# One pipe for both halves of a differential attention, and its rope and transposes allowed to start earlier

## The chip, the cores and the metric

The kernel runs on one core of one Trainium2 chip. The metric is device time in microseconds (us) of that core for one launch: the median of the runs shown. In the profile PE is TensorE (PEld its weight loads), DVE VectorE, ACT ScalarE, POOL GpSimd, and SP the engine that issues most of the DMAs.

## The reference, cut to what matters

The program computes two transformer blocks for 256 tokens of width 2048, all in fp32. What the change touches lies in the first block:

```python
h = rms_norm(x, g) * (1 + scale_a) + shift_a          # modulation from w_ada
proj = h @ w_in                                       # d_q d_k d_v | s_q s_k s_v | i_q i_k i_w
# differential attention: 8 heads, two 64-wide q/k per head, v 128 wide, causal, rope on q and k
p1 = softmax(mask(q1 @ k1.T) / 8);  p2 = softmax(mask(q2 @ k2.T) / 8)
diff_out = rms_norm((p1 - lam * p2) @ v, g_sub) * 0.2
# selected-key attention: 8 heads of 128 share one k and v; an index score picks 64 keys per query
dsa_out = softmax(where(selected, s_q @ s_k.T, -inf) / sqrt(128)) @ s_v
x = x + gate_a * rms_norm(concat(diff_out, dsa_out) @ w_o)
# then the gated feed-forward of this block, and the second block
```

## The kernel before, in words

**Weights.** Every projection streams its fp32 weights from HBM in pieces of up to 1 MB. A piece is loaded by SP into a buffer of a ring (`pump_dma`, L242 to L268); then, in units of two 128-row chunks, ACT copies it to a rounded part `wh` (L286) and DVE computes the rest `wl` (L287), and PE multiplies `hi*wh + hi*wl + lo*wh` (L327 to L329). A split is written at most `LOOK = 3` units ahead of the unit that PE works on (L273). The modulation needs `w_ada`, whose pieces PE reads as loaded (`ada`, L650); the planner deals them between the projections (`merge`, L349).

**The ring.** It has four fixed buffers (`raw0` to `raw3`) and up to `lent["max"]` more (tile name `rawb`), lent from the 14 big tiles (`slots`). A buffer comes back when its last unit is split, or when PE has read a modulation piece (`release`, L216). When a big tile is asked for and none is free, a lent one is reclaimed (L79).

**The order of the work.** Nothing is scheduled at run time: the Python program writes every engine's instructions in their final order, driven by a model clock that PE instructions advance (L64, L69). Side work (attention, evictions, norms) is written as generators that `yield` a model time until their next piece. `pipe` (L366) lays items through stages: item i reaches stage j at model time i*every + offs[j].

**The attentions.** `dsa_gen` (L897) sends 8 items (2 query tiles, 4 head pairs) through stages sA to sE; PE scores and adds the mask, DVE and ACT make the softmax, PE transposes `p` and multiplies with v. `diff_gen` (L961) waits for all of `dsa`, then, for each half q (4 heads), allocates and clears `kTz` (POOL memset, L1047), ropes `accA` on DVE (L1052), transposes k and q on PE (L1055, L1059) and evicts them to `kTz` and `dqT`, and sends 8 items through its seven stages: sA scores (`sc<-kTz,dqT`), sB softmax, sC the combination of p1 and p2 on DVE (L989, L990), sD transposes of `p`, sE the product with v (`tp<-accV,pt`), sF the norm, sG transposes of `osb`. The second half begins with nothing until the first pipe has drained and freed `kTz0`. Meanwhile PE works through the rest of `w_in` (tiles `h1h`, `h1l`), then `w_o`, first the selected-key rows (`mh`, `ml`), then the differential rows, which need `diff` (L1205).

Of the kernel before, what the change touches and what calls it, by code (L numbers as in the profile page):

```python
# [10 lines left out]
R32 = mybir.dt.float32r  # L11
BF = mybir.dt.bfloat16
I32 = mybir.dt.int32
AF = mybir.ActivationFunctionType
# [3 lines left out]
P = 128  # L18
# [21 lines left out]
def kernel(ctx: ExitStack, tc: tile.TileContext, a, freq, out):  # L40
# [30 lines left out]

    T = PE

    # ------------------------------------------------------------------ storage
    slots = deque(range(14))
    slot_of = {}

    def big(name, shape=(P, 8, 256), dt=F32):
        if not slots:  # L79
            reclaim()  # L80
        i = slots.popleft()
        t = bigp.tile(list(shape), dt, name=name, tag=f"b{i}")
        slot_of[name] = i
        return t

    def free(*names):
        for n in names:
            slots.append(slot_of.pop(n))
# [30 lines left out]
    def sc_bank():  # L119
        return psx.tile([P, 512], F32, name="sc", tag="sc", bufs=2)  # L120

    # ------------------------------------------------------------------ driver
    bg = []
    H = {}

# [9 lines left out]
    def spawn(gen, name=None):  # L135
        h = Handle()
        if name is not None:
            H[name] = h
        e = [gen, clock["t"], h]
        if step_gen(e):  # L140
            bg.append(e)
        return h
# [10 lines left out]
    def mark(name):  # L153
        H[name] = Handle()
        H[name].done = True
# [10 lines left out]
    def done(*names):  # L166
        return all(x in H and H[x].done for x in names)
# [29 lines left out]
                     "fin": u["last"] == i} for i, (u, ts) in enumerate(seq)]  # L197

    ring = deque(("raw", i) for i in range(N_RAW))
    lent = {"now": 0, "max": 0}  # L200

    def reclaim():
        for r in ring:
# [7 lines left out]
    def lend(n):  # L211
        lent["max"] = n
        while lent["now"] > n and reclaim():
            pass

    def release(it):  # L216
        ring.append(it["res"])
        lend(lent["max"])

    def run(steps):  # L220
# [21 lines left out]
        def pump_dma():  # L242
            while pos["dma"] < len(items):
                i = pos["dma"]
                it = items[i]
                if lent["now"] < lent["max"] and len(slots) > 0:
                    ring.append(("big", slots.popleft()))
                    lent["now"] += 1
                if not ring:
                    return  # L250
                it["res"] = ring.popleft()
                if it["res"][0] == "raw":
                    it["tile"] = rawp.tile([P, 2048], F32, name="raw", tag=f"raw{it['res'][1]}")
                else:
                    it["tile"] = bigp.tile([P, 2048], F32, name="rawb", tag=f"b{it['res'][1]}")
                if it["kind"] == "w":
                    g = it["grp"]
                    kcs = it["kcs"]
                    r0 = kcs[0] * P
                    src = g.w[r0:r0 + len(kcs) * P, g.c0:g.c0 + g.n].rearrange("(c p) n -> p c n", p=P)  # L260
                    it["view"] = it["tile"][:, :len(kcs) * g.n].rearrange("p (c n) -> p c n", n=g.n)
                    nc.sync.dma_start(it["view"], src)
                else:
                    it["load"](it["tile"])
                nb = 2048 if it["kind"] == "ada" else len(it["kcs"]) * it["grp"].n
                pos["t"] = max(pos["t"], clock["t"]) + nb * 512 / 361e3
                it["due"] = pos["t"] + DLAT
                pos["dma"] += 1  # L268
# [94 lines left out]
    def call(fn):  # L363
        return {"kind": "call", "fn": fn}

    def pipe(items, stages, offs, every):  # L366
        ev = sorted((i * every + offs[j], -j, i) for i in range(len(items)) for j in range(len(stages)))
        t = 0.0
        for tt, j, i in ev:
            if tt > t:  # L370
                yield tt - t
                t = tt
            stages[-j](items[i])

    # ------------------------------------------------------------------ constants
    v1 = wtile(tag="P", bufs=4, name="v1")
    v1 = v1[:, :P]
    rows = lambda v, n: v.rearrange("o (r c) -> (o r) c", c=P)[:n]
# [125 lines left out]
        V.tensor_scalar(nlam, nlam, 0.2, None, op0=OP.subtract)  # L504


    # ------------------------------------------------------------------ helpers
    def rstd_of(ssq, n, width, name="rstd"):
        k = ssq.shape[1]
        v = small(k, name + "v")  # L510
# [10 lines left out]
    def quad_transpose(src, pb=None):  # L521
        pb = pb if pb is not None else tp_bank()
        n = src.shape[1] // P
        for j in range(n):
            T.transpose(pb[:, j * P:(j + 1) * P], src[:, j * P:(j + 1) * P], ident)
        return pb[:, :n * P].rearrange("p (c q) -> p c q", q=P)
# [25 lines left out]
            A.activation(h, src, AF.Copy, scale=scale)  # L552
            V.scalar_tensor_tensor(l, src, scale, h, op0=OP.mult, op1=OP.subtract)

    # ------------------------------------------------------------------ modulation
    def ada_item(load, use, after=lambda: None):
        return {"kind": "ada", "item": {"kind": "ada", "load": load, "use": use}, "after": after}

# [158 lines left out]
                set_state("ada_free", True)  # L717
        return gen

    # ------------------------------------------------------------------ first norm  # L720
    ssx = cst.tile([P, 2, 4], F32, name="ssx")
    first = ada_chunk(0)
    firsts = []
# [25 lines left out]
    free("x0", "x1", "ada0", "ada1", "ada2", "ada3")  # L749
    hid["hi"], hid["lo"] = [big("h1h0", dt=R32), None], [big("h1l0", dt=R32), None]  # L750

    # ------------------------------------------------------------------ w_in of the first block
    acc = {}
    for q in range(2):
        acc["A", q] = big(f"accA{q}", (P, 2, 2, 512))
# [39 lines left out]
            s += g.steps()  # L795
        return s

    # index scores and the selection of keys
    iws = cst.tile([P, 2, 16], F32, name="iws")

    def idx_gen():
# [95 lines left out]
    def dsa_gen():  # L897
# [8 lines left out]
        def sA(it):  # L906
            t, p = it
            nk = P * (t + 1)
            b = sc_bank()
            b3 = b[:, :2 * nk].rearrange("p (j k) -> p j k", j=2)  # L910
            T.matmul(b3, negi, M[:, t, :nk][:, None, :].to_broadcast([P, 2, nk]), start=True, stop=False,
                     skip_group_check=True)
            for j in range(2):
                T.matmul(b3[:, j, :], sqT[:, 2 * p + j, t * P:(t + 1) * P], skT[:, :nk],
                         start=False, stop=True, skip_group_check=True)
            live[it] = b

        def sB(it):
            t, p = it
# [38 lines left out]
                        [0.0, 0.68, 2.38, 8.5, 10.79], 3.2)  # L958
        free("sqT", "accC0", "accC1")

    def diff_gen():  # L961
        while not done("dsa"):
            yield POLL
        kTz = {}
        dqT = big("dqT")
        scale = 64 ** -0.5
        live = {}

# [65 lines left out]
        def sG(it):  # L1034
            t, h = it
            if h % 4 != 3:
                return
            q = h // 4
            pb = quad_transpose(live.pop(("o", it)))
            hh = mh[:, 4 * q:4 * q + 4, t * P:(t + 1) * P]  # L1040
            A.activation(hh, pb, AF.Copy, scale=gdiff)
            V.scalar_tensor_tensor(ml[:, 4 * q:4 * q + 4, t * P:(t + 1) * P], pb, gdiff, hh, op0=OP.mult,
                                   op1=OP.subtract)

        for q in range(2):
            kTz[q] = big(f"kTz{q}", (P, 4, 2, 256))
            G.memset(kTz[q], 0.0)  # L1047
            while not done(f"win{512 * q}_d.1", f"win{1024 + 512 * q}_d.1"):
                yield POLL
            src = acc["A", q]  # L1050
            for t in range(2):
                rope(src[:, t].rearrange("p s (n d) -> p (s n) d", d=64)[:, :, 0:16], 16, t)  # L1052
            yield 7.0
            for t in range(2):
                pb = quad_transpose(src[:, t, 1, :])  # L1055
                A.activation(kTz[q][0:64, :, 0, t * P:(t + 1) * P], pb[0:64], AF.Copy)
                V.tensor_copy(kTz[q][64:128, :, 1, t * P:(t + 1) * P], pb[64:128])
                yield 1.89
                pb = quad_transpose(src[:, t, 0, :])  # L1059
                A.activation(dqT[:, 4 * q:4 * q + 4, t * P:(t + 1) * P], pb, AF.Copy)  # L1060
                yield 1.89
            free(f"accA{q}")
            if q == 0:
                mh, ml = big("mh0", dt=R32), big("ml0", dt=R32)
                hid["mh0"], hid["ml0"] = mh, ml
            while not done(f"win{2048 + 512 * q}_d.1"):
                yield POLL
            yield from pipe([(t, h) for t in range(2) for h in range(4 * q, 4 * q + 4)],
                            [sA, sB, sC, sD, sE, sF, sG],
                            [0.0, 1.12, 4.01, 9.5, 12.09, 13.2, 19.98], 2.64)  # L1070
            free(f"kTz{q}")
        set_state("sc_free", True)
        free("dqT", "accV")

# [11 lines left out]
        free_pair("h1")  # L1086

    def start_diff():
        spawn(diff_gen(), "diff")

    steps = []
# [20 lines left out]
    sd.insert(nd, call(start_diff))  # L1112
    steps += merge(sd, gate_a + shift_f)

    # ------------------------------------------------------------------ output of the attention
    mix_hi = lambda kc, t: (hid["mh%d" % (kc // 8)][:, kc % 8, t * P:(t + 1) * P],
                            hid["ml%d" % (kc // 8)][:, kc % 8, t * P:(t + 1) * P])
    w_o = a["w_o"][0]
# [91 lines left out]
    def after_o():  # L1210
        free("mh0", "ml0", "mh1", "ml1")

    # ------------------------------------------------------------------ feed-forward
    DFF = 5632
    w_gate, w_up, w_down = a["w_gate"][0], a["w_up"][0], a["w_down"][0]
    lhs2 = lambda kc, t: hilo_lhs(*hid["h2"])(kc, t)
# [103 lines left out]

    steps += fsteps[nf:]

    # ------------------------------------------------------------------ second block
    w_in2 = a["w_in_2"]
    lhs3 = lambda kc, t: hilo_lhs(*hid["h3"])(kc, t)
    need3 = lambda ks, t: [f"h3.{t}.{k // 4}" for k in ks]
# [58 lines left out]
    steps += Grp("ck0", w_in2, 512, 288, range(16), lhs3, post_ck0).steps()  # L1385
    steps += Grp("ck1", w_in2, 800, 288, range(16), lhs3, post_ck1).steps()

    # gated convolution
    C_IN, B_GATE, C_GATE, Z_CONV = 3136, 5184, 7232, 9280
    G_MLA, G_CONV, Z_MLA = 11328, 13376, 1088  # L1390
    uT = {}
# [360 lines left out]
```

## Time and profile before

| | us |
|---|---|
| median of 3 runs | 2367.16 (2366.83 to 2367.84) |
| profiled execution: span from the first to the last instruction | 2365.9 |
| PE busy in the span | 2315.8 (98%) |
| PE idle in the span, span less busy | 50.1 |
| DVE busy, ACT busy | 1306.1 (55%), 1069.0 (45%) |

A profiled execution is one run with every instruction recorded; its span ends within 1.3 us of the median of the runs, and the own time of that execution outside its span is not given. PE is the engine that is nearly always busy, so time is first of all sought in its idle stretches. Its busy time is modelled from starts and lengths, and matmuls overlap; how fast it works is read from the distance between starts.

### The profile page before, as it was taken

Reading aid. Unit: us, or ns where it says so; the run is one execution under the profiler, and the core shown is the slowest. Engines: PE = TensorE matmul, PEld = TensorE weight load, DVE = VectorE, ACT = ScalarE, POOL = GpSimd, SP = SyncE. Lnnn points to the kernel's source line nnn. Section 1 sums busy time; section 2 is a strip of 40 time slices with the busy share of each in tenths; the row PEclk is TensorE's granted clock in tenths of the full one; section 3 lists DMA queues with packets and bytes.
Section 4 is the critical chain, followed back from the end, with each engine's and each line's share of the span. In section 5 each row is a group of like instructions: output and inputs, shape, how many; then the busy total and the mean of one; then the engine's idle time right before and its main releaser. Section 6 shows DMA issues by size and latency. Waiting matters only on the chain.

```text
span 2365.9 us, 27898 instructions
## 1 busy us (share of the span) xinstructions
PE 2315.8 (98%) x11044; PEld 1842.3 (78%) x11044; DVE 1306.1 (55%) x1710; ACT 1069.0 (45%) x1503; POOL 96.8 (4%) x117
## 2 busy tenths in 40 slices
PE   7999999999999999999998999999999999999998
PEld 5666666677887888888887888888888988888887
DVE  3656756556664444554556655555544654554554
ACT  4434345546444444434444644444445544444443
POOL 1311011010000000000001000000000000000000
PEclk9999999999999999999999999999999999999999
DMA  9996888957775556556554665565565553565563
GB/s 302 330 320 237 318 309 301 318 209 277 242 261 191 191 192 195 179 196 195 186 188 144 220 195 190 179 200 188 179 204 161 168 171 125 172 219 196 187 204 125
DMA packets 237619, 506.57 MB, mean 214 GB/s; under 512 B 9288, under 2 KB 31984, under 8 KB 228400
## 3 DMA queue, kind: packets, MB, share of 16 engines
q1 hardware_dynamic: 235392, 496.14, 62.3%
q0 software_dynamic: 1872, 8.58, 1.1%
q8 instruction: 86, 1.41, 0.2%
q14 instruction: 45, 0.37, 0.0%
q10 hardware_dynamic: 224, 0.07, 0.0%
HBM read 500.56 MB, written 4.19 MB: 213 GB/s over the span
## 4 chain that ended last, share of the span: by engine, by line
PE 75%; DVE 1%; ACT 1%; issue 1%; POOL 0%; DVEq 0%; POOLq 0%; ACTq 0%
PE mm L65 71%; PE tp L70 1%; PE sc L65 1%; PE tp L65 1%; PE tpb L70 1%; DVE wl L287 0%; DVE xr L1155 0%; ACT h3h L1163 0%; DVE h3l L1166 0%; POOL rstd L513 0%; ACT wh L286 0%; ACT junk L1178 0%; DVE ot L1705 0%; ACT hm L1277 0%; DVE hm L1273 0%
## 5 line engine op out<-in xcount | busy, mean ns | idle before, releaser
L287 DVE TENSOR_TENSOR wl<-raw,wh 128x1024 fp32r<-128x1024 f32 (+3 forms) x723 | 871.9, 1212 | 766.5 <-ACT wh L286 760.4
L286 ACT ACTIVATE wh<-raw 128x1024 fp32r<-128x1024 f32 (+3 forms) x723 | 745.9, 1038 | 696.4 <-PE mm L65 686.3
L65 PE MATMUL mm<-wh,h3h 128*128 128x512 f32 (+1 forms) x992 | 387.1, 390 | 1.7 <-ACT h3h L1163 1.2
L65 PE MATMUL mm<-wl,h3h 128*128 128x512 f32 (+1 forms) x992 | 380.7, 384 | 0.4 <-DVE wl L287 0.4
L65 PE MATMUL mm<-wh,h3l 128*128 128x512 f32 (+1 forms) x992 | 381.0, 384 | 0.0
L65 PE MATMUL mm<-wh,h2h 128*128 128x512 f32 x704 | 276.3, 393 | 0.0
L65 PE MATMUL mm<-wl,h2h 128*128 128x512 f32 x704 | 274.6, 390 | 0.9 <-DVE wl L287 0.9
L65 PE MATMUL mm<-wh,h2l 128*128 128x512 f32 x704 | 274.7, 390 | 0.0
L65 PEld LDWEIGHTS mm<-wh,h3h 128*128 128x128 f32 x992 | 186.7, 188 | 37.8 <-ACT h3h L1163 1.6
L65 PEld LDWEIGHTS mm<-wh,h3l 128*128 128x128 f32 x992 | 186.5, 188 | 37.4 <-DVE h3l L1166 0.4
L65 PEld LDWEIGHTS mm<-wl,h3h 128*128 128x128 f32 x992 | 186.8, 188 | 34.8 <-DVE wl L287 0.6
L65 PE MATMUL mm<-wh,h1h 128*128 128x512 f32 (+2 forms) x384 | 154.0, 401 | 3.4 <-ACT wh L286 2.5
L65 PEld LDWEIGHTS mm<-wl,h2h 128*128 128x128 f32 x704 | 132.5, 188 | 28.1 <-DVE wl L287 1.2
L65 PEld LDWEIGHTS mm<-wh,h2h 128*128 128x128 f32 x704 | 132.5, 188 | 27.7 <-issue 0.8
L65 PEld LDWEIGHTS mm<-wh,h2l 128*128 128x128 f32 x704 | 132.4, 188 | 27.6
L65 PE MATMUL mm<-wl,h1h 128*128 128x512 f32 (+2 forms) x384 | 142.7, 372 | 7.8 <-DVE wl L287 7.8
L65 PE MATMUL mm<-wh,h1l 128*128 128x512 f32 (+2 forms) x384 | 142.0, 370 | 1.9 <-DVE h1l L627 1.9
L65 PE MATMUL mm<-wh,acth 128*128 128x512 f32 x352 | 139.3, 396 | 0.0
L65 PE MATMUL mm<-wh,actl 128*128 128x512 f32 x352 | 137.1, 390 | 0.0
L65 PE MATMUL mm<-wl,acth 128*128 128x512 f32 x352 | 137.0, 389 | 0.0
L65 PEld LDWEIGHTS mm<-wh,h1h 128*128 128x128 f32 x384 | 72.8, 190 | 55.7 <-issue 26.7
L65 PEld LDWEIGHTS mm<-wl,h1h 128*128 128x128 f32 x384 | 72.9, 190 | 21.2 <-DVE wl L287 10.9
(412 smaller groups left out, 2777.7 us busy)
## 6 DMA issues: line engine op xcount, KB each, us to landing
raw<-in_w_in_dram SPq DMA_DIRECT2D x134, 1024.0 KB, 5.2
raw<-in_w_ada_dram SPq DMA_DIRECT2D x47, 1024.0 KB, 4.9
raw<-in_w_gate_dram SPq DMA_DIRECT2D x44, 1024.0 KB, 5.3
raw<-in_w_up_dram SPq DMA_DIRECT2D x44, 1024.0 KB, 5.2
raw<-in_w_down_dram SPq DMA_DIRECT2D x44, 1024.0 KB, 5.1
raw<-in_w_ada_dram SPq DMA_DIRECT2D x36, 512.0 KB, 8.9
rawb<-in_w_ada_dram SPq DMA_DIRECT2D x17, 1024.0 KB, 6.5
raw<-in_w_o_conv_dram SPq DMA_DIRECT2D x16, 1024.0 KB, 5.1
```

The lines of the kernel that those rows point to most:

```text
L65: return nc.tensor.matmul(o, l, r, **kw)
L70: return nc.tensor.transpose(o, i, idn)
L286: A.activation(wh[:, :m, :g.n], src, AF.Copy)
L287: V.tensor_sub(wl[:, :m, :g.n], src, wh[:, :m, :g.n])
```

## The change

`diff_gen` no longer waits for the whole of `dsa` but for its last score matmul (`dsascores`), and for the preparation of its first half. The preparation of each half (allocation, memset, rope, transposes, evictions) is a generator of its own, `diff_prep(q)`, started at once for both halves. It may begin after `dsascores` for the first half and after `dsa` for the second. It gets its big tiles by `claim(n)`, which reclaims lent ring buffers as they come free, lets no new one be lent below the claimed number, and waits until n tiles are free. The two halves' 16 items go through one pipe; an item enters only when its half is prepared, its v columns are projected and the output tiles exist (`ready`).

```diff
+    def claim(n):
+        lent["claims"] += n
+        while True:
+            while len(slots) < n and reclaim():
+                pass
+            if len(slots) >= n:
+                break
+            yield POLL
+        lent["claims"] -= n
     def release(it):
+        if it["res"][0] == "big" and len(slots) < lent["claims"]:
+            slots.append(it["res"][1])
+            lent["now"] -= 1
+            return
-                if lent["now"] < lent["max"] and len(slots) > 0:
+                if lent["now"] < lent["max"] and len(slots) > lent["claims"]:
+            if ready is not None and j == 0:          # in pipe()
+                while not ready(items[i]):
+                    yield POLL
+            if it == (1, 3):                          # in the sA of dsa_gen
+                mark("dsascores")
+    def diff_prep(q):
+        while not done("dsa" if q else "dsascores", f"win{512 * q}_d.1", f"win{1024 + 512 * q}_d.1"):
+            yield POLL
+        yield from claim(2 if q == 0 else 1)
+        # dqT (once), kTz[q], memset, rope, transposes and evictions as they were in diff_gen
     def diff_gen():
-        while not done("dsa"):
+        while not done("dsascores", "diffprep0"):
             yield POLL
-        for q in range(2):
-            kTz[q] = big(f"kTz{q}", (P, 4, 2, 256))
...
-            yield from pipe([(t, h) for t in range(2) for h in range(4 * q, 4 * q + 4)],
+        yield from pipe([(t, h) for q in range(2) for t in range(2) for h in range(4 * q, 4 * q + 4)],
                         [sA, sB, sC, sD, sE, sF, sG],
-                        [0.0, 1.12, 4.01, 9.5, 12.09, 13.2, 19.98], 2.64)
+                        [0.0, 1.12, 4.01, 9.5, 12.09, 13.2, 19.98], 2.64, ready)
     def start_diff():
+        for q in range(2):
+            spawn(diff_prep(q), f"diffprep{q}")
         spawn(diff_gen(), "diff")
```

Where PE finishes the first half's query tile 0 (`tp<-accV,pt`), there stood before the transposes of `p` of query tile 1, between the matmuls of the last `w_in` group (`h1h`, `h1l`; `ada` is a piece of the modulation):

```order
L65 MATMUL tp<-accV,pt 128x128 x4
L70 MATMUL tp<-ident,p 128x128 x2
L65 MATMUL ada<-raw,csil 32x512 x4
L65 MATMUL mm<-wh,h1h_1395 128x512
L65 MATMUL mm<-wl,h1h_1395 128x512
L65 MATMUL mm<-wh,h1l_1396 128x512
L65 MATMUL mm<-wh,h1h_1395 128x512
L65 MATMUL mm<-wl,h1h_1395 128x512
L65 MATMUL mm<-wh,h1l_1396 128x512
L70 MATMUL tp<-ident,p 128x128 x2
```

and now the second half's transposes (`accA`) come in between:

```order
L65 MATMUL ada<-raw,csil 32x512 x4
L65 MATMUL tp<-accV,pt 128x128 x4
L70 MATMUL tp<-ident,p 128x128 x2
L70 MATMUL tp<-ident,accA_266 128x128 x4
L65 MATMUL mm<-wh,h1h_1395 128x512
L65 MATMUL mm<-wl,h1h_1395 128x512
L65 MATMUL mm<-wh,h1l_1396 128x512
L65 MATMUL mm<-wh,h1h_1395 128x512
L65 MATMUL mm<-wl,h1h_1395 128x512
L65 MATMUL mm<-wh,h1l_1396 128x512
L70 MATMUL tp<-ident,accA_266 128x128 x4
```

The second half's four transposes begin 82 rows further up than before, and the last transposes of `osb`, with which the attention ends on PE, stand 77 rows further up. The first half's four stand where they stood, and so does everything on PE behind the old end of the attention. PE has the same instructions in both programs.

On SP, whose list holds the loads, the third and fourth pieces of the last-but-one `w_in` group and of the modulation stood like this (`rawb` is a lent buffer):

```order
L262 DMA raw<-in_w_in_dram 128x4x512
L642 DMA raw<-in_w_ada_dram 128x2048
L262 DMA rawb<-in_w_in_dram 128x4x512
L642 DMA raw<-in_w_ada_dram 128x2048 x2
L262 DMA rawb<-in_w_in_dram 128x4x512
L642 DMA raw<-in_w_ada_dram 128x2048
L642 DMA rawb<-in_w_ada_dram 128x2048
L262 DMA raw<-in_w_in_dram 128x4x512
```

and now so:

```order
L276 DMA raw<-in_w_in_dram 128x4x512
L659 DMA raw<-in_w_ada_dram 128x2048
L276 DMA raw<-in_w_in_dram 128x4x512
L659 DMA raw<-in_w_ada_dram 128x2048
L659 DMA rawb<-in_w_ada_dram 128x2048
L276 DMA rawb<-in_w_in_dram 128x4x512
L659 DMA raw<-in_w_ada_dram 128x2048 x2
L276 DMA raw<-in_w_in_dram 128x4x512
```

The loads keep their order, but the third one shown no longer has a lent buffer: it takes the fixed buffer that the fourth had, and the fourth that of the fifth.

## Rows read from the trace of the kernel before

**Rows 1.** The page's first part: busy time, share and instructions of each engine.

```profile
span 2365.9 us, 27898 instructions
PE 2315.8 (98%) x11044; PEld 1842.3 (78%) x11044; DVE 1306.1 (55%) x1710; ACT 1069.0 (45%) x1503; POOL 96.8 (4%) x117
```

**Rows 2.** PE's waits between 200 and 500: total us, times, longest.

```profile
PE mm L65 <- DVE wl L287: 2.5, 3, 1.2
PE tp L70 <- DVE ikd L807: 0.2, 1, 0.2
```

**Rows 3.** Stretches, all engines: length, busy (instructions) each, PEclk, DMA share, GB/s.

```profile
340.00:480.00 140.00, 140.00 (x738) 87.57 (x737) 80.68 (x178) 68.67 (x147) 13.66 (x11) 1.00 0.88 320
500.00:520.00 20.00, 20.00 (x90) 16.58 (x89) 12.39 (x11) 9.16 (x15) 5.07 (x4) 1.00 0.60 209
520.00:540.00 20.00, 14.62 (x94) 9.09 (x92) 11.64 (x26) 10.00 (x26) 4.21 (x8) 0.99 0.60 216
```

**Rows 4.** PE's waits between 500 and 560.

```profile
PE tp L65 <- ACT hm L1192: 3.1, 1, 3.1
PE tp L65 <- DVE dg L1181: 2.2, 1, 2.2
```

**Rows 5.** PE's instructions in order of time: start, us, instruction, xcount.

```profile
363.19 1.06 PE L65 MATMUL ada<-raw,csil 128*32 128x512 f32 x8
...
369.26 0.48 PE L65 MATMUL mm<-wh,h1h 128*128 128x512 f32 x1
369.57 0.40 PE L65 MATMUL mm<-wl,h1h 128*128 128x512 f32 x1
369.81 0.40 PE L65 MATMUL mm<-wh,h1l 128*128 128x512 f32 x1
...
377.52 0.27 PE L70 MATMUL tp<-ident,p 128*128 128x128 f32 x1
...
389.73 0.38 PE L70 MATMUL tp<-ident,p 128*128 128x128 f32 x2
```

**Rows 6.** DVE in order of time.

```profile
347.41 0.41 DVE L428 TENSOR_TENSOR ra<-accA,rcos 128x256 f32<-128x256 f32 x1
...
349.46 0.43 DVE L431 TENSOR_TENSOR accA<-ra,rb 128x256 f32<-128x256 f32 x1
...
374.88 0.35 DVE L990 SCALAR_TENSOR_TENSOR p<-p,rs 128x128 f32<-128x128 f32 x1
...
382.29 0.48 DVE L990 SCALAR_TENSOR_TENSOR p<-p,rs 128x256 f32<-128x256 f32 x1
```

**Rows 7.** SP's DMA issues in order of time.

```profile
337.25 0.39 SPq L262 DMA_DIRECT2D rawb<-in_w_in_dram  x1
341.31 4.91 SPq L642 DMA_DIRECT2D raw<-in_w_ada_dram  x2
346.31 2.24 SPq L262 DMA_DIRECT2D rawb<-in_w_in_dram  x1
...
385.68 0.38 SPq L642 DMA_DIRECT2D rawb<-in_w_ada_dram  x1
391.17 0.38 SPq L262 DMA_DIRECT2D raw<-in_w_o_dram  x1
394.47 0.33 SPq L642 DMA_DIRECT2D rawb<-in_w_ada_dram  x1
```

**Rows 8.** DMA issues of 335 to 405: xcount, KB, median us to landing.

```profile
raw<-in_w_ada_dram SPq DMA_DIRECT2D x10, 1024.0 KB, 5.7
rawb<-in_w_in_dram SPq DMA_DIRECT2D x2, 1024.0 KB, 8.0
```

**Rows 9.** ACT's splits in order of time, first and last of six.

```profile
347.56 1.06 ACT L286 ACTIVATE wh<-rawb 128x1024 fp32r<-128x1024 f32 x1 [0.79 <-PE mm L65]
...
372.06 1.05 ACT L286 ACTIVATE wh<-raw 128x1024 fp32r<-128x1024 f32 x1
```

**Rows 10.** PE's modulation matmuls alone, stretch: length, PE, PEld, ACT busy, PEclk, DMA share, GB/s.

```profile
340.00:480.00 140.00, 28.75 (x216) 4.23 (x216) 0.60 (x1) 1.00 0.88 320
```

More of the change, by code (lines that the diff above doesn't have):

```diff
@@ L199 @@
     ring = deque(("raw", i) for i in range(N_RAW))
-    lent = {"now": 0, "max": 0}
+    lent = {"now": 0, "max": 0, "claims": 0}
     def reclaim():
@@ L364, in call, with pipe @@
         return {"kind": "call", "fn": fn}
-    def pipe(items, stages, offs, every):
+    def pipe(items, stages, offs, every, ready=None):
         ev = sorted((i * every + offs[j], -j, i) for i in range(len(items)) for j in range(len(stages)))
@@ L959, in dsa_gen @@
         free("sqT", "accC0", "accC1")
+    kTz = {}
+    def diff_prep(q):
+        while not done("dsa" if q else "dsascores", f"win{512 * q}_d.1", f"win{1024 + 512 * q}_d.1"):
+            yield POLL
+        yield from claim(2 if q == 0 else 1)
+        if q == 0:
+            hid["dqT"] = big("dqT")
+        dqT = hid["dqT"]
+        kTz[q] = big(f"kTz{q}", (P, 4, 2, 256))
+        G.memset(kTz[q], 0.0)
+        src = acc["A", q]
+        for t in range(2):
+            rope(src[:, t].rearrange("p s (n d) -> p (s n) d", d=64)[:, :, 0:16], 16, t)
+        yield 7.0
+        for t in range(2):
+            pb = quad_transpose(src[:, t, 1, :])
+            A.activation(kTz[q][0:64, :, 0, t * P:(t + 1) * P], pb[0:64], AF.Copy)
+            V.tensor_copy(kTz[q][64:128, :, 1, t * P:(t + 1) * P], pb[64:128])
+            yield 1.89
+            pb = quad_transpose(src[:, t, 0, :])
+            A.activation(dqT[:, 4 * q:4 * q + 4, t * P:(t + 1) * P], pb, AF.Copy)
+            yield 1.89
+        free(f"accA{q}")
     def diff_gen():
-        while not done("dsa"):
+        while not done("dsascores", "diffprep0"):
             yield POLL
-        kTz = {}
-        dqT = big("dqT")
+        dqT = hid["dqT"]
         scale = 64 ** -0.5
@@ L1039, in sG @@
             pb = quad_transpose(live.pop(("o", it)))
+            mh, ml = mhml
             hh = mh[:, 4 * q:4 * q + 4, t * P:(t + 1) * P]
@@ L1043, in sG, with ready, outputs @@
                                    op1=OP.subtract)
-        for q in range(2):
-            kTz[q] = big(f"kTz{q}", (P, 4, 2, 256))
-            G.memset(kTz[q], 0.0)
-            while not done(f"win{512 * q}_d.1", f"win{1024 + 512 * q}_d.1"):
-                yield POLL
[L1050 to L1067, printed above, removed]
-            yield from pipe([(t, h) for t in range(2) for h in range(4 * q, 4 * q + 4)],
-                            [sA, sB, sC, sD, sE, sF, sG],
-                            [0.0, 1.12, 4.01, 9.5, 12.09, 13.2, 19.98], 2.64)
-            free(f"kTz{q}")
+        mhml = []
+        def ready(it):
+            q = it[1] // 4
+            if not done(f"diffprep{q}", f"win{2048 + 512 * q}_d.1"):
+                return False
+            return bool(mhml)
+        def outputs():
+            while not done("dsa"):
+                yield POLL
+            yield from claim(2)
+            hid["mh0"], hid["ml0"] = big("mh0", dt=R32), big("ml0", dt=R32)
+            mhml.extend((hid["mh0"], hid["ml0"]))
+        spawn(outputs())
+        yield from pipe([(t, h) for q in range(2) for t in range(2) for h in range(4 * q, 4 * q + 4)],
+                        [sA, sB, sC, sD, sE, sF, sG],
+                        [0.0, 1.12, 4.01, 9.5, 12.09, 13.2, 19.98], 2.64, ready)
+        free("kTz0", "kTz1")
         set_state("sc_free", True)
```

## The prediction

> **What bounds the kernel now.** I read the page's first part first: PE is busy for 2315.8 of 2365.9 us, so no change on another engine shortens anything unless PE stops waiting [rows 1]. Then I asked where PE's 50 us of idle time lie, and whether any lie where the change works. PE's waits between 200 and 500 are two rows, together 2.7 us [rows 2]. The stretch in which the differential attention runs, 340 to 480, has 140.00 us of PE in 140 us, so none of those 2.7 us is in it [rows 3]. The next idle time comes at 520 to 540, where PE is busy for 14.62 of 20 us [rows 3]; it waits there for `hm` and `dg`, 5.3 us [rows 4], the norm between the attention's output and the feed-forward, long after the attention. So in the stretch that the change rewrites there is no PE wait to take away. The granted clock there is 1.00 of the higher level, 2.4 GHz, so nothing is lost to the clock either [rows 3].
>
> What is nearly full beside PE is the weight stream: 320 GB/s and a DMA share of 0.88 over the stretch, against 209 GB/s and 0.60 at 500 to 520, when the attention is over [rows 3]. That is what a careless change could hurt.
>
> **The change, part by part.**
>
> *PE's own work.* Nothing is added or removed: the order of PE has 9639 rows in both programs, with the same operations. The first half's transposes keep their place; the second half's move 82 rows up, the end of the attention 77 rows up; behind it everything stands as before. What can differ is the price of switching between the weight matmuls and other work: the first weight matmul behind an attention instruction leads the next by 0.31 us (369.26 to 369.57), the following one by 0.24 [rows 5], so 0.07 us a switch. I counted the returns to weight matmuls in the order over the 500 rows around the change: 46 before, 45 after. That gives -0.07 us; if the moved pieces cost ten switches more or fewer than I count, 0.7 us either way. I take 0.
>
> *The wait for the selected-key attention* (a looser condition). The first half's preparation may now begin after the last score matmul, but it must claim two big tiles, and by the order its transposes still stand where they stood: the two lent ring buffers that it would reclaim come back no earlier than the attention frees its own tiles. So this part moves nothing on PE: 0 us.
>
> *The second half's preparation inside the first half's pipe.* Its rope is eight DVE operations from 347.41 to the end of the one at 349.46, 2.5 us in one piece for the first half [rows 6]; the second half's is of the same shapes. Before, the burst stood where no pipe ran; now it stands before the pending combinations of the first half. Bound from below: 0, if the items behind it have more margin than 2.5 us. From above: the tightest item seen, whose p is ready on DVE at 374.88 + 0.35 = 375.23 and is transposed at 377.52 [rows 5, 6], has 2.3 us; a burst before it would cost PE 0.2 us, and if each of the four items of query tile 1 had that margin and were hit anew, 0.8. The items actually in work are those of query tile 1, of which the one ready at 382.29 + 0.48 = 382.77 is transposed at 389.73 [rows 5, 6]: 7.0 us. The row nearest to the case is this one: I take 0, and keep 0.8 for the range. If that cover were gone, each further microsecond of delay would be a microsecond of PE.
>
> *The claims on the ring.* This is the part that could cost. The first claim takes both lent buffers while the selected-key attention ends. The load that went out at 337.25 into a lent buffer now takes the fixed buffer that came free for the one at 341.31, 4.1 us later; that one takes the second of the pair at 341.31, which goes out about 4.6 us later; the load at 346.31 finds the attention's old tiles free and goes out as before [rows 7]. Queued behind these on SP are only other loads. The second claim (one tile, `kTz1`) takes a lent buffer again while the second half is prepared: the modulation piece that went out at 385.68 moves to about 391.17, 5.5 us, and the weights of 391.17 to about 394.47, 3.3 us [rows 7]. Largest delay: 5.5 us.
>
> What hides it: a modulation piece issued at 341.31 lands after a median of 5.7 us [rows 7, 8] and, pieces and matmuls being paired in order, is multiplied at 363.19 [rows 5]: 363.2 - 347.0 = 16.2 us of margin. For weights the splits stand up to three units ahead of PE; six splits in 347.56 to 372.06 are 4.9 us a unit [rows 9], so 14.7 us, less the split itself (1.06 us on ACT [rows 9] and, as an estimate, as much on DVE): 12.5 us from landing to use even if a piece lands only as its split begins. The one of 337.25 lands after some 8.0 us, at 345.3 [rows 8], 2.3 us before its split at 347.56 [rows 9]; 4.1 us later it would keep ACT and the DVE split behind it waiting for 1.8 us, inside the 12.5. So 0 us on PE; the cost if the cover is gone is in the second rival.
>
> *The longer stretch behind the attention* is freed of it 77 rows earlier; PE's work there is the same and already without a gap. 0 us.
>
> The sum is 0 against the span of 2365.9 us of the profiled execution [rows 1]. The median of the runs, 2367.16, lies 1.3 us above it, time outside the span that the change does not touch. Forecast: 2367.2 us, its own range 2366.0 to 2369.0 (0.7 us of switches and a little of the runs' spread below, 0.7 + 0.8 us and a late load above).
>
> **A rule against this reading.** Over 340 to 480 PE shows no gap, but its weight loads are busy for 87.57 of 140 us, 63%, against 16.58 of 20, 83%, at 500 to 520 [rows 3]. The Trainium skill (Perfetto Trace Analysis, Identifying the Most-Contended Engine) says that the busy share of matmuls is no good measure of how close TensorE is to its roofline, and that the busy share of weight loads is a better one. By it the stretch would have 140 x (1 - 62.6/82.9) = 34 us of headroom, an estimate, and the sum could be far below 0. The trace agrees only in part: 28.75 of the 140 us are the modulation's matmuls, with 4.23 us of weight loads [rows 10]; without them the share is 83.3 of 111.25, 75%. Most of the difference is thus other work, not room, and the change keeps all of that work.
>
> **The rivals.**
>
> *The ring starves PE: slower.* For: the stream runs at 0.88 [rows 3], so lost buffers are not won back quickly. A buffer turns in 363.19 + 1.06 - 341.31 = 22.9 us [rows 5, 7]. Two are missing for 337.25 to 346.31, 9.1 us, and one for the second half's preparation, some 16 us (347.41, the first half's rope, to 363.19, when its pipe runs [rows 5, 6]): (2 x 9.1 + 16)/22.9 = 1.5 pieces of 1 MB not loaded in time, at 320 GB/s 3.3 us each, 4.9 us. If the margins above are used up, all of it is PE's: 2367.2 + 4.9 = 2372.1 us. It decides once a load is more than some 12.5 us late at its split. Against: the largest shift I find is 5.5 us, and the two claims are 48 us apart (337 to 385), in which the spare 12% of the stream, 5.8 us, makes good the first. Chance 0.11.
>
> *The wait behind the attention shrinks: faster.* DVE and ACT are done with the attention earlier, and the norm chain that PE waits for (5.3 us [rows 4]) could start with emptier queues; or the denser order lets PE use some of the headroom that the weight loads' share hints at. If the whole wait went: 2367.2 - 5.3 = 2361.9 us. Against: the stretch of the attention ends 40 us before that of the wait [rows 3], and the operations waited for hang on the last output matmul, which stays where it is. Chance 0.06.
>
> *The change does less than it says.* It holds in part already (the first half does not move); if the second half's move is also without effect, the time is the forecast's, so it takes no chance from it.
>
> **How the numbers follow.** The forecast has 0.83, the slower rival 0.11, the faster one 0.06. Differences of under 0.2%, 4.7 us, count as no change, about what a measurement of this kernel can tell. The forecast's own range lies within it; the rivals at 2372.1 and 2361.9 just outside, and smaller versions of both inside. So: faster 0.05, same 0.84, slower 0.11. The range reaches a little to both sides of the forecast's own, further up than down since a half of the starved ring (2.5 us) fits the unknowns: 2364.5 to 2371.0.
>
> **What would show it.** In the profile after: PE without a gap over 340 to 480, as now; the second half's `accA` transposes some 20 us or more before their old place, and the last `osb` transposes likewise; the same wait of about 5 us for `hm` and `dg`. Wrong would be: PE waits for `wl` or `wh` in the stretch, with ACT waiting for DMA landings before them (the ring); PE waits for `p` or `osb` behind DVE (the burst); or a changed wait at 520 to 540 (the faster rival).

## The result: 0.55% slower, and the profile after

| | before | after |
|---|---|---|
| median of the runs, us | 2367.5 (2366.83 to 2367.97, 4 runs) | 2379.67 (2378.35 to 2382.50, 4 runs) |
| ratio to before, 95% interval | | 1.0055 (1.0041 to 1.0069) |
| span of the profiled execution, us | 2365.9 | 2376.6 |

The forecast was 2367.2 us with 2371.0 as the upper end of its range; the kernel became 12.2 us slower. The profiled execution took 2378.35 us, the fastest of the four, so it shows a little less than the median does.

The stretch that answers to [rows 3], and three of its pieces, from the changed kernel's windows (columns: window, us; busy time of PE, PEld, DVE, ACT, POOL; granted clock, DMA share, GB/s):

```profile
340.00:480.00 140.00, 131.88 (x686) 82.70 (x684) 76.88 (x176) 64.12 (x143) 12.94 (x11) 0.99 0.77 289
396.00:400.00 4.00, 1.92 (x7) 1.73 (x8) 1.44 (x7) 2.50 (x8) 0.00 (x0) 0.67 0.74 252
400.00:404.00 4.00, 4.00 (x22) 3.27 (x21) 2.33 (x7) 1.31 (x3) 1.05 (x1) 0.90 0.05 16
440.00:444.00 4.00, 1.35 (x11) 1.35 (x12) 3.18 (x10) 1.77 (x6) 0.00 (x0) 1.00 0.99 369
```

PE had no gap in these 140 us before; now it is idle for 8.1 of them, and for a few microseconds behind the first gap it works at a lower clock. What it waits for between 200 and 500, the view of [rows 2]:

```profile
PE tp L70 <- ACT osb L1060: 5.1, 1, 5.1
PE tp L65 <- ACT pt L1045: 3.1, 2, 2.6
PE mm L65 <- DVE wl L301: 2.5, 3, 1.2
...
```

The third row is the 2.5 us of before; the first two are new. Both name an eviction by ScalarE (ACT), its copy of what stands in a `tp` bank, a PSUM buffer in which transposes and the products with `accV` land. Neither wait had a price in the prediction's sum. PE's timeline at the two places:

```profile
390.96 0.94 PE L65 MATMUL tp<-accV,pt 128*128 128x128 f32 x6
392.31 0.49 PE L65 MATMUL tp<-accV,pt 128*128 128x128 f32 x2 [0.41 <-ACT pt L1045]
392.64 0.38 PE L70 MATMUL tp<-ident,p 128*128 128x128 f32 x2
398.08 1.11 PE L70 MATMUL tp<-ident,accA 128*128 128x128 f32 x4 [5.06 <-ACT osb L1060]
...
399.42 0.63 PE L65 MATMUL mm<-wl,h1h 128*128 128x512 f32 x1
399.85 0.63 PE L65 MATMUL mm<-wh,h1l 128*128 128x512 f32 x1
...
442.65 1.16 PE L65 MATMUL tp<-accV,pt 128*128 128x128 f32 x8 [2.65 <-ACT pt L1045]
```

There are two `tp` banks. The product with `accV`, begun at 390.96, fills one, and the transpose of `p` at 392.64 the other. The next instruction in PE's order is the second half's first `accA` transpose. It is the third user, needs the product's bank back, and PE, which works in order, stands until that bank is copied to `osb`. All the weight products behind it stand too. After the gap those products are 0.43 us apart (399.42 to 399.85), against 0.24 in [rows 5]: the lower clock.

Why the copy is late is in ACT's and DVE's timelines. ACT, at both places:

```profile
392.14 2.01 ACT L300 ACTIVATE wh<-raw 128x1024 fp32r<-128x1024 f32 x2
396.52 0.47 ACT L894 ACTIVATE p<-sc,nm 128x256 f32<-128x256 f32 x1 [2.37 <-DVE rs L1030]
...
397.43 0.59 ACT L1060 ACTIVATE osb<-tp 128x512 f32<-128x512 f32 x1
...
437.60 1.07 ACT L300 ACTIVATE wh<-rawb 128x1024 fp32r<-128x1024 f32 x1
440.83 0.47 ACT L894 ACTIVATE p<-sc,nm 128x256 f32<-128x256 f32 x1 [2.16 <-DVE rs L1030]
...
441.74 0.69 ACT L1085 ACTIVATE mh<-tp,gdiff 128x512 fp32r<-128x512 f32 x1
442.31 0.28 ACT L1045 ACTIVATE pt<-tp 128x128 f32<-128x128 f32 x1
```

DVE, at both places:

```profile
393.24 2.36 DVE L301 TENSOR_TENSOR wl<-raw,wh 128x1024 fp32r<-128x1024 f32 x2 [1.24 <-ACT wh L300]
395.51 0.68 DVE L888 TENSOR_REDUCE nm<-sc 128x2 f32<-128x512 f32 x1
...
438.70 1.23 DVE L301 TENSOR_TENSOR wl<-rawb,wh 128x1024 fp32r<-128x1024 f32 x1 [1.71 <-ACT wh L300]
439.84 0.69 DVE L888 TENSOR_REDUCE nm<-sc 128x2 f32<-128x512 f32 x1
```

Read backwards: PE starts at 398.08 when `osb` ends (397.43 + 0.59 = 398.02). `osb` stands on ACT behind the two Exp of the next item, which wait for its maximum `nm` on DVE (395.51). That maximum stands on DVE behind the two subtractions `wl` of the weight splits (393.24), and these wait for ACT's two `wh` (392.14). The second place has the same chain with one split: `wh` 437.60, `wl` 438.70, `nm` 439.84, Exp 440.83, `mh`, then `pt` ends at 442.59 and the product starts at 442.65. All eight rows of that product wait, while at the first place six of eight start ahead of a late `pt` and only the last two wait for it (0.41 us). So the second stop, too, looks like one for a bank, not for the data; a4 below bears on this.

In the kernel before, the same product and its next two users of `tp` banks stood thus on PE (the transpose between them, at 389.73, is in [rows 5]):

```profile
388.84 1.05 PE L65 MATMUL tp<-accV,pt 128*128 128x128 f32 x8
...
390.04 1.06 PE L65 MATMUL ada<-raw,csil 128*32 128x512 f32 x8
...
392.54 0.38 PE L70 MATMUL tp<-ident,p 128*128 128x128 f32 x2
```

and on ACT:

```profile
387.22 1.06 ACT L286 ACTIVATE wh<-rawb 128x1024 fp32r<-128x1024 f32 x1
...
391.38 0.59 ACT L1017 ACTIVATE osb<-tp 128x512 f32<-128x512 f32 x1
...
392.12 1.07 ACT L286 ACTIVATE wh<-rawb 128x1024 fp32r<-128x1024 f32 x1
```

There eight modulation rows and six weight matmuls stood between the second user and the third, and `osb` ended 0.57 us before the third came (391.97 to 392.54). That small margin was what the absence of gaps rested on.

The change moved the splits on ACT too. Counted from 342 on, the eleventh and the twelfth `wh` stood at 387.22, ahead of the product, and at 392.12, behind `osb`. In the changed kernel both stand at 392.14, behind the start of the product and ahead of `osb`. So the third user came sooner, and the eviction that it needs came later: `osb` starts 2.5 us behind the start of the product before (388.84 to 391.38) and 6.5 us after (390.96 to 397.43). What in the new order moved these two splits is not shown.

**The account.** The same stretch of the program can be measured in both traces: from the end of a wait for `wl` at 210 to the moment at which PE begins to wait for `dg`. Of before:

```profile
210.32 0.39 PE L65 MATMUL mm<-wl,h1h 128*128 128x256 f32 x1 [1.17 <-DVE wl L287]
...
530.38 1.16 PE L65 MATMUL tp<-dg,xr 128*128 128x128 f32 x8 [2.15 <-DVE dg L1181]
```

and after:

```profile
211.33 0.39 PE L65 MATMUL mm<-wl,h1h 128*128 128x256 f32 x1 [1.17 <-DVE wl L301]
...
541.38 1.16 PE L65 MATMUL tp<-dg,xr 128*128 128x128 f32 x8 [2.17 <-DVE dg L1221]
```

530.38 - 2.15 - 210.32 = 317.91 us before and 541.38 - 2.17 - 211.33 = 327.88 after, 9.97 us more. The waits give 5.1 + 3.1 = 8.2, and the lower clock (0.33 + 0.10) x 4 = 1.7 us, together 9.9. The clock's part is an estimate, since the first of these pieces holds idle time too. The rest of the difference of the spans, 0.7 us, is outside this stretch.

### The profile page after: what moved, and what is told of

The parts are those of the page before. It is cut to its first block, busy times and chain, and to the rows that moved or that the text cites. A ratio compares the mean times of both kernels' runs of the same rounds, so it can differ in the third digit from the quotient of the medians.

```text
span 2376.6 us, 27892 instructions
## 1 busy us (share of the span) xinstructions
PE 2318.9 (98%) x11044; PEld 1842.7 (78%) x11044; DVE 1305.5 (55%) x1710; ACT 1068.8 (45%) x1503; POOL 96.2 (4%) x117
## 4 chain that ended last, share of the span: by engine, by line
PE 74%; DVE 1%; ACT 1%; issue 1%; POOL 0%; DVEq 0%; POOLq 0%; ACTq 0%
PE mm L65 71%; PE tp L70 1%; PE sc L65 1%; PE tp L65 1%; PE tpb L70 1%; DVE wl L301 0%; DVE xr L1195 0%; ACT h3h L1203 0%; ACT wh L300 0%; DVE h3l L1206 0%; ACT junk L1218 0%; DVE ot L1745 0%; ACT hm L1317 0%; DVE hm L1313 0%; POOL rstd L530 0%
```

## The experiments

Theory A: PE stops at a transpose bank, or for what is in one, because ACT's eviction stands behind splits and behind an Exp that DVE releases late. Rivals: the ring (loads that come late), the rope's burst on DVE, the bank count alone. The table gathers all runs. "Stretch" is the measure above, less 317.91; "waits" are PE's from 340 to 500; "clock" is what granted clocks under 0.97 cost, summed over pieces of 4 us from 380 to 520 as above. Medians and intervals are against runs of the kernel before on the same chip (2367.11 to 2367.50).

| kernel | median, us | ratio (95%) | stretch | waits | clock |
|---|---|---|---|---|---|
| after | 2379.67 | 1.0055 (1.0041 to 1.0069) | +10.0 | 8.2 | 1.7 |
| a1_prep_later | 2374.01 | 1.0027 (1.0016 to 1.0038) | +6.2 | 3.7 | 1.7 |
| a2_rope_first | 2380.13 | 1.0055 (1.0038 to 1.0071) | +13.0 | 8.1 | 5.1 |
| a3_two_pipes | 2374.83 | 1.0033 (1.0021 to 1.0045) | +8.6 | 5.5 | 3.4 |
| b1_ring | 2367.63 | 1.0000 (0.9991 to 1.0009) | 0.0 | 0 | 0 |
| b2_third_user | 2370.32 | 1.0013 (1.0004 to 1.0023) | +4.2 | 1.9 | 1.7 |
| a4_shared_banks | 2375.85 | 1.0036 (1.0022 to 1.0050) | +7.6 | 5.0 | 1.7 |
| a5_shared_slower_pipe | 2381.22 | 1.0056 (1.0041 to 1.0071) | +13.2 | 8.8 | 3.4 |
| a6_slower_pipe | 2379.43 | 1.0052 (1.0037 to 1.0067) | +12.5 | 7.9 | 3.4 |
| c1_splits_off | 2367.86 | 1.0001 (0.9993 to 1.0010) | +0.6 | 0.5 | 0 |
| c0_before_splits_off | 2367.33 | 1.0001 (0.9992 to 1.0010) | 0.0 | 0 | 0 |
| c2_two_pipes_prep_later | 2370.68 | 1.0015 (1.0006 to 1.0024) | +6.0 | 3.7 | 1.7 |

In every row waits and clock together come within 1.2 us of the stretch. "Stretch", "waits" and "clock" are of the one profiled execution of each kernel. The time ahead of the stretch differs between executions as well (it begins at 208.95 us in a3 and at 212.00 in c0), so the stretch and the median need not agree to the microsecond.

**One edit of the change at a time.** The second half's transposes 5 us later:

```diff
-        yield 7.0
+        yield 12.0 if q else 7.0
```

> The changed kernel, but the second half's transposes begin 12.0 instead of 7.0 of model time after its rope; on PE 18 weight matmuls and one modulation group (about 5.2 us) then stand between the first half's product with v and them, the rope stays where it is. Theory A (two transpose banks: PE stops at the accA transposes until ACT has evicted osb, which stands behind two splits and the next item's exponentials): the wait of 5.1 us before them falls under 0.5 us, and the low clock behind it with it; about 2373 us (2379.7 - 5.1 - 1.7), the wait of 2.6 us before the second half's product may stay. Theory B (ring: loads late by up to 5.5 us delay ACT and DVE): 2379.7 +- 1.5, since the loads go out as before. Theory C (the rope's burst on DVE): 2379.7 +- 1.5, since the burst is in its place.

```profile
PE tp L70 <- ACT pt L1045: 2.6, 1, 2.6
PE tp L70 <- DVE kTz L998: 0.7, 1, 0.7
...
```

As theory A has it, the wait of 5.1 us is gone, and of 12.2 us 5.5 come back. The one of 2.6 stays in size, but it is now at 437 and before a transpose of `p`, not before the product, and a low clock of 1.7 us follows it; so the time is 1 us above the expected 2373.

The rope taken out of the claimed part, ahead of the claim, with PE's order unchanged:

```diff
+        src = acc["A", q]
+        for t in range(2):
+            rope(...)
         yield from claim(2 if q == 0 else 1)
```

> The changed kernel, but the rope of a half runs before it claims its tiles, so the burst of eight DVE operations of the second half comes some 15 us earlier; PE's order is that of the changed kernel word for word. Theory C: the 5.1 us wait shrinks by the 2.5 us of the burst or more, 2377 us or less. Theories A and B: the wait stays at 5.1 +- 1 us, 2379.7 +- 1.5.

```profile
PE tp L70 <- ACT osb L1060: 4.0, 1, 4.0
PE tp L65 <- ACT pt L1045: 2.6, 1, 2.6
PE sc L65 <- DVE p L1033: 1.5, 1, 1.5
```

The burst moves, one microsecond of the first wait goes, and 1.5 us appear before a score product. The sum of the waits is the same and the time too: the burst is not the cause. In its profiled execution the low clock costs 3.4 us more than in the changed kernel's, and yet the execution is no longer (2378.03 against 2378.35 us); the time ahead of the stretch was 2.3 us shorter and that behind it 1.1 us.

Two pipes, as before, with the second half's preparation still overlapped:

```diff
-        yield from pipe([(t, h) for q in range(2) for t in range(2) ...
+        for q in range(2):
+            yield from pipe([(t, h) for t in range(2) ...
```

> The changed kernel, but with one pipe for each half, the second begun when the first has drained; the second half's preparation still overlaps the first pipe. Theory A: the wait before the accA transposes stays (5.1 us and the low clock behind it), the one of 2.6 us, where stages of both halves stand between each other on ACT, goes: about 2377 us. Theory B: 2379.7 +- 1.5.

```profile
PE tp L70 <- ACT osb L1060: 5.1, 1, 5.1
PE tp L65 <- ACT pt L1045: 0.4, 1, 0.4
```

Here the 2.6 us are gone and the 5.1 stay; the median is 2.2 us below the expected 2377. With a1, each wait goes with one edit taken singly: the 5.1 us with the place of the second half's transposes, the 2.6 us with the joined pipe. The last run below shows that the two do not simply add.

**From the other side.** The kernel before, with its ring giving up buffers where the change does:

```diff
+            if it == (1, 3):
+                lend(0)
...
+        lend(2)
         dqT = big("dqT")
...
+            if it == (0, 1):
+                lend(1)
```

> The kernel before, but the ring gives up its lent buffers as the change makes it: both from the last score matmul of the selected-key attention until that ends, and one from the middle of the first half's pipe until the output projection; PE's order is that of the kernel before word for word. Theory A: 2367.5 +- 1, no wait of PE between 340 and 480. Theory B: the change's loss returns, 2372 us or more, with PE waits in that stretch.

No wait of PE from 340 to 500, and no change of time: the ring is not the cause. The two splits keep their places (387.12 and 392.02), so the ring's shift alone did not move them either. And in the changed kernel's own trace ACT waits for no load between 330 and 480.

The kernel before with a third user of the banks put behind the product (four transposes of `accV`'s columns, copied to a tile that nothing reads):

```diff
+            if it == (1, 0):
+                px = quad_transpose(acc["V"][:, 0, 0:512])
+                A.activation(wtile(name="junk")..., px, AF.Copy)
```

> The kernel before, with one thing added: behind the first half's product with v and the next transposes of p, four more transposes (of v columns, result unused) take a transpose bank and ACT evicts them, as the second half's do in the changed kernel. Their own work on PE is about 0.6 us. Theory A (two banks): PE, done with what precedes them at about 390.1, stops until ACT has evicted osb at about 392.0, a wait of 1.5 to 2.5 us: 2369.5 to 2371 us, a little more if the clock falls. If the banks are not the cause: no wait, 2368.0 us.

```profile
389.63 0.38 PE L70 MATMUL tp<-ident,p 128*128 128x128 f32 x2
391.95 0.66 PE L70 MATMUL tp<-ident,accV 128*128 128x128 f32 x4 [1.94 <-ACT osb L1020]
```

The wait appears in the kernel before as well, for the same eviction, and the clock fell behind it (0.61 at 392 to 396). It is shorter than after the change: here `osb` starts 2.6 us behind the start of the product (388.74 to 391.30), there 6.5 us (390.96 to 397.43), with both splits in between. As an estimate, 1.9 of the 5.06 us are thus the price of the third user's place with the splits where they were, and the other 3.1 go with the splits' new place.

**More banks, a slower pipe.** The scores and the transposes share four banks in turn while the pipe runs, with PE's order unchanged:

```diff
-        return psx.tile([P, 512], F32, name="tp", tag="tp", bufs=2)
+        if state["share"]:
+            return psx.tile([P, 512], F32, name="tp", tag=next_bank())
```

> The changed kernel, but during the differential pipe scores and transposes take turns in all four banks of the two, instead of two each; the order of every engine is the changed kernel's. Theory A: the accA transposes no longer need the bank of the product just before, so their wait of 5.1 us falls under 0.5 and with it the low clock: about 2373 us; the wait of 2.6 us before the second half's product is for data (pt), not for a bank, and stays. Theories B and C: 2379.7 +- 1.5, the wait stays.

```profile
PE tp L70 <- ACT p L907: 2.7, 1, 2.7
PE tp L65 <- ACT p L907: 1.9, 1, 1.9
PE tp L65 <- ACT pt L1059: 0.4, 1, 0.4
```

The first four `accA` transposes no longer wait. The next four wait 2.7 us, where under 0.5 was expected, for a bank that an Exp reads; that Exp stands on ACT ahead of `osb` and behind the same two splits. The time is 2.9 us above the expected 2373. At the second place the product waits 1.9 us for an Exp and then starts at 438.99, ahead of its last `pt` at 439.40. So there, against the expectation, its start needs a bank and not the data. The Trainium skill (Perfetto Trace Analysis, Matmuls) advises rotating independent groups through different PSUM banks, so that evacuating one overlaps the next. This run agrees in part: more banks help by 2.4 us at the first place, but all of them wait for one late engine.

The same with a pitch of 3.3 us instead of 2.64, and the slower pitch alone:

```diff
-  [0.0, 1.12, 4.01, 9.5, 12.09, 13.2, 19.98], 2.64, ready)
+  [0.0, 1.12, 4.01, 9.5, 12.7, 13.8, 20.6], 3.3, ready)
```

> As the one before, and the pipe takes an item every 3.3 instead of 2.64 of model time, with the product with v 3.2 instead of 2.6 behind the transposes of p, so that PE reaches it later than ACT has evicted pt. If the second wait is PE arriving early at an eviction that stands behind a weight split and the next item's exponentials: both waits fall under 1 us and the time returns to the kernel before's, 2368 +- 1.5 us. If the change costs by something beside these waits: 2370 us or more with no wait in the stretch.

> The changed kernel with that slower pipe alone, two banks each. The accA transposes now stand both before and behind the first product with v. Theory A: a bank wait of 1 to 5 us stays near them, the wait for pt before the second product goes: 2371 to 2376 us. If pace alone is the cause (DVE and ACT too dense): 2368 +- 1.5 us.

Waits of the first of the two:

```profile
PE tp L70 <- ACT p L907: 5.9, 2, 3.1
...
```

The shared banks with the slower pipe missed what I expected by 13 us, and the slower pitch alone, expected at 2371 to 2376 us, is as slow as the change itself. A slower pitch does not widen each margin; it puts every item at another place among the splits, and new waits for ACT and DVE, of up to 3.1 us in a5 and 2.4 in a6, arise there. That is against pace as the cause and fits the order on ACT and DVE, which the next runs test.

**Taking away what stands ahead of the evictions.** GpSimd fills `wh` and `wl` with a constant while the pipe runs, so the splits leave ACT and DVE (the weights of these products are then not the real ones). PE's order, the two banks and the pipe stay, and the loads keep their order; but nothing reads the weights loaded for these products, so that a load can go out sooner (the one of 395.62 at 391.59):

```diff
+                if hid.get("cut"):
+                    G.memset(wh[...], 0.015625)
+                    G.memset(wl[...], 0.00006103515625)
+                else:
                     A.activation(wh[:, :m, :g.n], src, AF.Copy)
                     V.tensor_sub(wl[:, :m, :g.n], src, wh[:, :m, :g.n])
```

> The changed kernel with its splits of weights taken off ScalarE and VectorE while the one pipe runs: 17 times GpSimd fills wh and wl with a constant instead of ScalarE copying and VectorE subtracting, so the weights of those products are not the real ones. TensorE's order, the two transpose banks, the pipe and the ring stay those of the changed kernel. Theory A (TensorE stops at a transpose bank because ScalarE's eviction of it stands behind splits and behind an Exp that VectorE releases late): the waits of 5.1 and 2.6 us shrink to 0 to 1.3 and 0 to 0.5 us, the clock stays at its upper level, 2367.5 to 2370.0 us, though every transpose stands where it stood. Rival R (two banks are too few for this order of transposes, whoever evicts them, or something else of the change costs the time): the waits and 2377 to 2381 us stay.

The same in the kernel before, as a control; the edit meets 17 splits in the changed kernel and 22 here, from the first pipe's start to the second's end:

> The kernel before with the same 22 splits replaced while its two pipes run, as a control for c1_splits_off: the weights of those products are not the real ones. Theory A: TensorE has no wait there to lose, 2367.2 us within 1.2. If ScalarE's and VectorE's load costs time in another way than by the waits at the transpose banks, it falls below 2366.

The changed kernel without the splits, its stretch and its one wait:

```profile
340.00:480.00 140.00, 139.53 (x733) 87.54 (x731) 67.54 (x161) 50.52 (x129) 44.00 (x45) 1.00 0.83 313
```

```profile
PE tp L70 <- ACT osb L1064: 0.5, 1, 0.5
```

and ACT at the first place:

```profile
391.30 0.47 ACT L898 ACTIVATE p<-sc,nm 128x256 f32<-128x256 f32 x1 [1.92 <-DVE rs L1034]
...
392.28 0.60 ACT L1064 ACTIVATE osb<-tp 128x512 f32<-128x512 f32 x1
```

`osb` now starts at 392.28 instead of 397.43; the 5.1 us have become 0.5, the second wait is gone, the clock stays at its upper level, and the whole 0.55% comes back (1.0001). The kernel before gains nothing by the same relief. So PE's order and the two banks alone cost next to nothing; they cost time because the splits make the evictions late. That is shown for the splits as a whole; that the sooner loads are not what helps rests on b1 and on ACT's waits in the changed kernel, which name no load. Which share is ACT's and which is DVE's was not tried. By the timelines of the first place, of the 4.4 us from the first `wh` (392.14) to the Exp (396.52), 1.1 pass until the first `wl` starts, 2.3 in the two `wl`, and 1.0 in DVE's steps from `nm` to the Exp.

**Both single cures together** (two pipes, and the transposes 5 us later):

> The changed kernel with both single edits that took away one wait each: two pipes (that took away the wait at 442) and the second half's transposes 5 us later (that took away the one at 398); the rope and transposes of the second half still overlap the selected-key attention and the first pipe. Theory A with waits that belong to two separate places: 0.4 to 1.5 us of waits are left, 2367.5 to 2369.5 us. Rival M (the waits move to whatever transpose stands close in the new order, as they did with the slower pipe): 2 to 6 us of waits at other transposes, and 2371 to 2377 us.

```profile
PE tp L70 <- ACT osb L1060: 2.3, 1, 2.3
...
```

The time, 2370.68 us, lies between the two expectations; the 3.7 us of waits are those of rival M. The two old waits of 5.1 and 2.6 us are gone, but a transpose of `p` now waits 2.3 us for `osb`, which stands at 397.57 behind the same two splits. Its profiled execution was its slowest (2374.27 us), so its stretch and waits may be above those of the median run. No version beats the kernel before, and in a stretch where PE has no gap none was to be expected.

## Why the prediction was wrong

*What bounds the kernel*: right. PE was full, and there was nothing to win; what I did not ask was how nearly it was not full. The 1.3 us taken for time outside the span was short, the profiled execution after the change shows 1.75 (2378.35 less 2376.6); the forecast does not turn on it.

*PE's own work*, 0: right. With the splits off the changed order needs 0.6 us more for the stretch than the order before, 0.5 of it the remaining wait.

*The wait for the selected-key attention*, 0: right. The first half's first `accA` transposes stand at 355.06 instead of 354.03, and 1.01 us of that is there already at 211.33.

*The second half's preparation inside the first half's pipe*, 0 with 0.8 as the upper bound: this step failed, at the 5.1 us. I judged it by one margin, how long `p` is ready on DVE before PE transposes it, 2.3 to 7.0 us, and by one new load, the rope's burst. I did not count that the preparation also brings four groups of transposes, that each takes one of two banks, and that its place in PE's order follows directly on two other users. The margin that mattered was the 0.57 us between ACT's `osb` and the third user of the bank; it is in the trace of before, on ACT's timeline, which I did not use. Nor did I ask whether the splits would keep their places on ACT; both now stand between the product's start and `osb`, and by the estimate from b2 that is the larger part of the wait. Moving the burst left the time as it was (a2), moving the transposes removed the wait (a1), a third user in the kernel before brought one (b2), and taking the splits away from ACT and DVE removed it in place (c1).

The same omission covers the joined pipe, which I did not cost at all beyond its switches. It brings the second wait, 2.6 us: the product with `accV` stops until ACT has evicted a late `pt`. Before, the same product came 0.62 us behind the end of its last `pt` (452.78 less 451.88 + 0.28):

```profile
452.78 1.05 PE L65 MATMUL tp<-accV,pt 128*128 128x128 f32 x8
```

```profile
451.88 0.28 ACT L1002 ACTIVATE pt<-tp 128x128 f32<-128x128 f32 x1
```

*The claims on the ring*, 0: right, with its shifts. SP's issues in the changed kernel, which comes to this part of the program 1.0 us later:

```profile
342.34 0.38 SPq L276 DMA_DIRECT2D raw<-in_w_in_dram  x1
346.93 0.33 SPq L659 DMA_DIRECT2D raw<-in_w_ada_dram  x1
...
391.09 0.33 SPq L659 DMA_DIRECT2D raw<-in_w_ada_dram  x1
395.62 0.38 SPq L276 DMA_DIRECT2D raw<-in_w_o_dram  x1
```

They answer to the issues at 337.25, 341.31, 385.68 and 391.17 of [rows 7]: 4.1, 4.6, 4.4 and 3.4 us later once the 1.0 is taken off, against the 4.1, 4.6, 5.5 and 3.3 that I gave. No wait of PE for a weight is added, and b1 gives 1.0000.

*The lower clock* had no term: 1.7 us here, by the estimate above. I wrote that nothing is lost to the clock, which held only as long as there was no gap.

*The rule on the busy share of weight loads*: no run shows the room of 34 us that it would give; no order tried ran the stretch in less than 317.9 us.

*The signs that I named*: the second half's first `accA` transposes came 21.4 us earlier (419.46 to 398.08), as forecast; the last `osb` transposes came 11.6 us earlier (476.59 to 465.03), not some 20, with the waits and the low clock ahead of them; and the 5.3 us for `hm` and `dg` stayed (3.1 + 2.2).

*The rivals*: the slower one had the right sign and the wrong cause (no weight came late). My list of what would prove me wrong named PE waiting for `osb`, but "behind DVE (the burst)"; it is behind ACT and the splits. Since I saw only the ring as a way to lose, I gave slower too small a chance.

## What to carry to other kernels

Before costing moved transposes or products at nothing, list the users of their PSUM banks in TensorE's order, and for each the place of the eviction on its engine and the time left: in a stretch without gaps the smallest of these margins (here 0.57 us) is the number to know. An eviction is as late as everything ahead of it in its engine's queue, so a split or an Exp that was harmless behind it can stop TensorE ahead of it. A new order on TensorE can move those too, as it moved the two splits here; list their places again after the change. To test such a cause, leave the order alone and relieve the evicting engine: if the time returns, the order was not too tight in itself.

## What the runs showed of the hardware

A short stop of TensorE cost more than itself at most of the places. Behind the gap of 5.06 us the granted clock was 0.67 and 0.90 in the next pieces of 4 us, with weight products 0.43 us apart, and behind only 1.94 us (b2) it was 0.61 and 0.96. Yet the gap of 2.65 us at 442 left it at 1.00, while one of 2.6 us at 437 (a1) was followed by 0.81 and 0.76, and gaps of 0.5 to 0.7 us by nothing. By the pieces of 4 us such a drop cost 1.7 us in most runs and 3.4 in a3 and a6 and at the first place of a2, where a whole piece stood at half the clock, 1.2 GHz (a3: 0.86, 0.50, 0.79). What decides between these was not tried.
